# Scan of a Mamba-2 layer: the loads of the cumulated step sizes, one for each chunk, issued from ScalarE's queue rather than SyncE's

## The chip, the core and the metric

The kernel runs on one core of one Trainium2 chip. The metric is the device time of one execution in microseconds (us). The engines have these short names: PE is TensorE (matrix products), PEld its weight load, DVE is VectorE, ACT is ScalarE, POOL is GpSimd, SP is SyncE, which here does nothing but issue DMAs ("SPq" in the profile is its queue of issues).

## The reference

One inference step of a decoder trunk of two layers: a Mamba-2 SSD layer and a pooling layer, each with adaLN modulation, RMSNorm and a gate, on 1024 prompt tokens and 8 sequences of 8 sample tokens (1088 columns in all), model width 1024. The change lies in the scan of the SSD layer, which has 32 heads of 64 channels in 8 groups of 4 heads, a state of 128, and chunks of 128 tokens:

```python
def ssd_scan(x, dt, A, B, C, h0):
    ...
    acum = jnp.cumsum(dt * A.reshape(G, R), axis=2)          # per chunk: the cumulated step sizes
    seg = acum[:, :, :, None] - acum[:, :, None, :]
    decay = jnp.where(mask, jnp.exp(jnp.where(mask, seg, 0.0)), 0.0)
    CB = jnp.einsum('bctgn,bcsgn->bctsg', C, B)
    xdt = x * dt[..., None]
    y_intra = jnp.einsum('bctsgr,bcsgrp->bctgrp', CB[..., None] * decay, xdt)
    decay_end = jnp.exp(acum[:, :, -1:] - acum)
    chunk_states = jnp.einsum('bctgn,bctgr,bctgrp->bcgrpn', B, decay_end, xdt)
    chunk_decay = jnp.exp(acum[:, :, -1])
    # h <- chunk_decay * h + chunk_states, chunk by chunk, h_prev = the h ahead of each chunk
    y_inter = jnp.einsum('bctgn,bctgr,bcgrpn->bctgrp', C, jnp.exp(acum), h_prev)
    return y_intra + y_inter, h_final
```

All of it is float32. Products that must be exact to float32 are made as three products of high and low halves.

## The kernel before

**The scan.** Function `scan_group(g, T)` does one of the 8 head groups: 8 chunks of 128 prompt tokens, two at a time, and a ninth, shorter chunk with the 64 sample tokens. The cumulated step sizes of all heads lie in DRAM (`acd`, written once before the scan). For each chunk, `load_ac(c)` brings those of the group's 4 heads to the core, the same numbers to all 128 partitions, into a tile `acb` (128 x 4 x 128 float32, 256 KB; 128 KB for the ninth chunk). There are two buffers for `acb`. `front(c)` takes the tile of its chunk and first issues the load of the next chunk, which goes to the other buffer and so waits until the last reader of the chunk before is done. All readers of `acb` are on ACT: `ea` = exp(acb) (L543), four `M` = relu(tka - acb) (L556), and `cd` = exp of acb's last column (L574, only chunks 1 to 7). Beside them `front` transposes x and B on PE (L545, L549, tile `tr`), turns M into the decay matrix (ACT L557, DVE L559 and L560), makes `xd` (DVE L562), the copy `Bt` of the transposed B (ACT L566; L569 and L570 for the ninth chunk), and multiplies `ea` by C (DVE L575). `states` makes the chunk states `S` of two chunks on PE (L588, from `Bt` and `xd`) and carries the state on: `hd` = h x cd on POOL (L596), `h` = hd + S on DVE (L593, L597). `rows` makes the outputs on PE: L609 from `M`, L613 from `ea` and `h`; DVE adds them up (L580). The sample tokens follow (L617 to L667: `Z` L628, `st` L652 and L653, `xs` L660, S L663, store `hsT` L666), then the gate (`z` loads L512, L700, L701), the norm (L706 to L716, with a store `rsd` and a load `rs`) and the store of the result (`gyd`, L723).

**What runs beside it.** PE always has other products to make in between: the input projection of the next groups (`mm`, L182 to L184, a weight tile `wr` is loaded by SP at L117 to L123, split into `wh` by ACT at L139 and `wl` by DVE at L140; results are taken out by ACT at L419, the convolution is at L356 to L360), the adaLN vectors (`am` L253 and L262, with `mp` copied by ACT at L258), and, from the fifth group on, the output projection of the groups that are done (`gr` loaded at L737, split into `gh` by ACT L742 and `gl` by DVE L743; the running sum `x` is loaded at L1521, added to at L764, and stored as `x1d` at L1544). The table `FILL` says how many pieces of this other work are written between two steps of a scan.

**What sets the order.** The program is written once through this code, and a scheduler then gives each engine one fixed list of instructions. An engine works its list from the top: an instruction whose inputs or buffers aren't there holds up all that stands behind it on that engine. That holds for the DMAs too: a DMA stands in the list of the engine that issues it. The DMAs of SP and of ACT share eight completion semaphores, DMAHW0 to DMAHW7, which are given out in turn, and a DMA can be issued only when the DMA that had its semaphore before has landed. Before the change ACT issues no DMA; SP issues all of this stage.

Of the kernel before, what the change touches and what calls it, by code (L numbers as in the profile page):

```python
# [14 lines left out]
P = 128  # L15
# [82 lines left out]
class Build:  # L98
# [405 lines left out]
    def scan_group(self, g, T):  # L504
        nc, tk, gp, pp = self.nc, self.tk, self.gs, self.pp
# [18 lines left out]
        def load_ac(c):  # L524
            if c < 8:
                j, cc = c // 2, c % 2
                t = gp.tile([P, 4, 128], F32, tag="acb", bufs=2, name=self.name("acb"))
                nc.sync.dma_start(t, self.acd[32 * j + 4 * g:32 * j + 4 * g + 4, 128 * cc:128 * cc + 128].unsqueeze(0).to_broadcast([P, 4, 128]))
            else:
                t = gp.tile([P, 4, 128], F32, tag="acb", bufs=2, name=self.name("acb"))[:, :, :64]  # L530
                nc.sync.dma_start(t, self.acd[96 + 4 * g:100 + 4 * g, 256:320].unsqueeze(0).to_broadcast([P, 4, 64]))
            acbs[c] = t

        def front(c):
# [4 lines left out]
            tok = slice(t0, t0 + L)  # L539
            acb = acbs.pop(c)  # L540
            load_ac(c + 1) if c < 8 else None
            ea = gp.tile([P, 4, 128], F32, tag="ea", bufs=3, name=self.name("ea"))
            nc.scalar.activation(ea[:, :, :L], acb, AF.Exp)  # L543
# [112 lines left out]
        def state_sample(st, Bt, half):  # L656
# [10 lines left out]
            self.slots.free(hsl[half])  # L667

        load_ac(0)
        F = [front(0)]  # L670
        yield
# [1135 lines left out]
```

## Time and profile before

| | |
|---|---|
| median of 3 runs (lowest to highest) | 1624.79 us (1623.5 to 1626.45) |
| profiled execution, its own time | 1625.1 us |
| its span | 1623.2 us |
| granted TensorE clock, mean | 0.995 |
| PE busy / ACT busy, share of the span | 98% / 50% |
| the scan stage | about 355 to 930 us |
| loads of `acb` | 64 of 256 KB and 8 of 128 KB |

The span is the time from the first to the last instruction on the core; the execution's own time adds some 2 us around it. In the rows that follow, "busy" is the time in which an engine worked on an instruction, and a wait is the idle time of an engine ahead of an instruction, put down to the instruction or DMA that ended last of those it waited for. Waits of SPq are waits of the queue of issues.

### The profile page before, as it was taken

How to read it: one execution, taken by the hardware profiler on the slowest of the kernel's cores; microseconds unless marked ns; L12 is line 12 of the kernel's file. 1: busy time of each engine (PE TensorE's matmuls, PEld its weight loads, DVE VectorE, ACT ScalarE, POOL GpSimd, SP SyncE). 2: the span in 40 equal slices, each digit the busy share in tenths (PEclk: the TensorE clock that was granted, in tenths of full speed). 3: DMA queues.
4: the chain of work that ended last, by engine and by line, in shares of the span. 5: the costliest groups of instructions: out<-in, count | busy, mean ns of one | idle time of the engine just before them, and what ended most of it. 6: DMA issues, size and time to landing. Idle time of an engine off the chain costs nothing.

```text
span 1623.2 us, 30975 instructions
## 1 busy us (share of the span) xinstructions
PE 1594.8 (98%) x12061; PEld 1519.9 (94%) x12061; DVE 1290.4 (79%) x2140; ACT 815.2 (50%) x1565; POOL 497.8 (31%) x527
## 2 busy tenths in 40 slices
PE   8999999999999999999999999999999999999997
PEld 6899999998889898898899899999999999999997
DVE  6875779777787888889878867988899867577886
ACT  6653444357667667675555536632322233333364
POOL 0233556421221302120112222366667640000241
PEclk9999999999999999999999999999999999999999
DMA  9422232354554554678899633043333369665773
GB/s 348 163 99 82 94 110 71 107 198 128 194 161 159 166 190 134 215 226 295 272 333 313 216 130 112 29 143 111 103 108 100 134 206 362 181 159 182 160 175 121
DMA packets 122306, 275.60 MB, mean 170 GB/s; under 512 B 18192, under 2 KB 59312, under 8 KB 122160
## 3 DMA queue, kind: packets, MB, share of 16 engines
q1 hardware_dynamic: 118128, 260.91, 47.4%
q0 software_dynamic: 4032, 12.72, 4.5%
q8 instruction: 95, 1.56, 0.4%
q14 instruction: 51, 0.42, 0.1%
HBM read 201.12 MB, written 70.23 MB: 167 GB/s over the span
## 4 chain that ended last, share of the span: by engine, by line
PE 83%; DVE 6%; DMA 4%; issue 3%; ACT 3%; POOL 1%; SPq 0%; DVEq 0%; POOLq 0%; ACTq 0%
PE st L982 11%; PE st L980 11%; PE st L981 11%; PE mm L182 10%; PE mm L183 10%; PE mm L184 10%; PE op L1197 2%; PE op L1198 2%; PE op L1196 2%; PE y L609 2%; PE S L588 2%; PE y L613 1%; DMA acb<-acd 1%; PE am L253 1%; PE tr L549 1%
## 5 line engine op out<-in xcount | busy, mean ns | idle before, releaser
L982 PE MATMUL st<-hh,w 128*128 128x272 f32 x832 | 240.8, 289 | 2.3 <-DVE w L176 2.3
L980 PE MATMUL st<-hh,w 128*128 128x272 f32 x832 | 240.2, 289 | 0.0
L981 PE MATMUL st<-hl,w 128*128 128x272 f32 x832 | 239.8, 288 | 0.0
L982 PE MATMUL st<-t,w 128*128 128x272 f32 x624 | 179.5, 288 | 0.0
L980 PE MATMUL st<-t,w 128*128 128x272 f32 x624 | 179.5, 288 | 0.0
L981 PE MATMUL st<-t,w 128*128 128x272 f32 x624 | 179.2, 287 | 0.0
L182 PE MATMUL mm<-hh,wh 128*128 128x368 f32 (+1 forms) x528 | 178.2, 338 | 0.1
L183 PE MATMUL mm<-hl,wh 128*128 128x368 f32 (+1 forms) x528 | 173.4, 328 | 0.0
L184 PE MATMUL mm<-hh,wl 128*128 128x368 f32 (+1 forms) x528 | 173.4, 328 | 0.0
L174 ACT ACTIVATE w<-wr 128x512 fp32r<-128x512 f32 x104 | 65.7, 631 | 190.1 <-PE st L982 156.7
L982 PEld LDWEIGHTS st<-hh,w 128*128 128x128 f32 x832 | 156.4, 188 | 3.4 <-DVE w L176 3.4
L980 PEld LDWEIGHTS st<-hh,w 128*128 128x128 f32 x832 | 156.7, 188 | 0.3 <-issue 0.3
L981 PEld LDWEIGHTS st<-hl,w 128*128 128x128 f32 x832 | 156.8, 188 | 0.0
L596 POOL TENSOR_TENSOR hd<-h,cd 128x256 f32<-128x256 f32 x56 | 48.7, 870 | 347.8 <-DVE h L597 190.5
L182 PE MATMUL mm<-gh,wh 128*128 128x368 f32 (+1 forms) x384 | 129.1, 337 | 0.6 <-ACT raw L419 0.6
L1197 PE MATMUL op<-b,w 128*128 128x272 f32 x448 | 128.9, 288 | 0.7 <-DVE b L1126 0.7
L1196 PE MATMUL op<-b,w 128*128 128x272 f32 x448 | 129.4, 289 | 0.0
L1198 PE MATMUL op<-b,w 128*128 128x272 f32 x448 | 128.9, 288 | 0.0
L183 PE MATMUL mm<-gl,wh 128*128 128x368 f32 (+1 forms) x384 | 126.0, 328 | 1.1 <-DVE gl L743 1.0
L184 PE MATMUL mm<-gh,wl 128*128 128x368 f32 (+1 forms) x384 | 126.0, 328 | 0.0
L980 PEld LDWEIGHTS st<-t,w 128*128 128x128 f32 x624 | 117.7, 189 | 0.0
L982 PEld LDWEIGHTS st<-t,w 128*128 128x128 f32 x624 | 117.3, 188 | 0.0
(293 smaller groups left out, 4610.4 us busy)
## 6 DMA issues: line engine op xcount, KB each, us to landing
wr<-win SPq DMA_DIRECT2D x48, 512.0 KB, 3.9
acb<-acd SPq DMA_DIRECT2D x64, 256.0 KB, 4.0
wr<-pin SPq DMA_DIRECT2D x32, 512.0 KB, 3.8
wr<-pout SPq DMA_DIRECT2D x28, 512.0 KB, 3.9
x<-x1d SPq DMA_DIRECT2D x24, 544.0 KB, 6.6
x1d<-x SPq DMA_DIRECT2D x22, 544.0 KB, 5.5
wr<-pout POOLq DMA_DIRECT2D x20, 512.0 KB, 5.5
x<-xT SPq DMA_DIRECT2D x16, 544.0 KB, 6.1
```

The costliest lines, as they stand in the source:

```text
L174: self.nc.scalar.activation(hi, src, AF.Copy)
L182: nc.tensor.matmul(ps[:, :n], hi[:, k, :], ah[:, a:a + n], start=first, stop=False)
L183: nc.tensor.matmul(ps[:, :n], hi[:, k, :], al[:, a:a + n], start=False, stop=False)
L184: nc.tensor.matmul(ps[:, :n], lo[:, k, :], ah[:, a:a + n], start=False, stop=last)
L588: nc.tensor.matmul(S[:, 256 * i:256 * i + 256], Bt, xde.rearrange("p r q -> p (r q)"), start=True, stop=True)
L596: nc.gpsimd.tensor_tensor(out=hd, in0=h[-1], in1=cd.unsqueeze(2).to_broadcast([P, 4, 64]), op=ALU.mult)
L980: nc.tensor.matmul(ps[c][:, :QUART], hi[:, k], xh[:, t], start=(k == 0), stop=False)
L981: nc.tensor.matmul(ps[c][:, :QUART], hi[:, k], xl[:, t], start=False, stop=False)
L982: nc.tensor.matmul(ps[c][:, :QUART], lo[:, k], xh[:, t], start=False, stop=(k == 3))
L1196: nc.tensor.matmul(ps[:, :QUART], hi[:, k], xh, start=k == 0, stop=False)
L1197: nc.tensor.matmul(ps[:, :QUART], hi[:, k], xl, start=False, stop=False)
L1198: nc.tensor.matmul(ps[:, :QUART], lo[:, k], xh, start=False, stop=k == 7)
```

## The change

In `load_ac` the two DMAs are issued by ACT:

```diff
 def load_ac(c):
     if c < 8:
         j, cc = c // 2, c % 2
         t = gp.tile([P, 4, 128], F32, tag="acb", bufs=2, name=self.name("acb"))
-        nc.sync.dma_start(t, self.acd[32 * j + 4 * g:32 * j + 4 * g + 4, 128 * cc:128 * cc + 128].unsqueeze(0).to_broadcast([P, 4, 128]))
+        nc.scalar.dma_start(t, self.acd[32 * j + 4 * g:32 * j + 4 * g + 4, 128 * cc:128 * cc + 128].unsqueeze(0).to_broadcast([P, 4, 128]))
     else:
         t = gp.tile([P, 4, 128], F32, tag="acb", bufs=2, name=self.name("acb"))[:, :, :64]
-        nc.sync.dma_start(t, self.acd[96 + 4 * g:100 + 4 * g, 256:320].unsqueeze(0).to_broadcast([P, 4, 64]))
+        nc.scalar.dma_start(t, self.acd[96 + 4 * g:100 + 4 * g, 256:320].unsqueeze(0).to_broadcast([P, 4, 64]))
     acbs[c] = t
```

The 72 issues go from SP's list to ACT's (L528 and L531), and the scheduler arranges the lists of this stage anew; outside the stage the order stays. Of the three places shown here, each named by the time at which it lies in the profile before, the first is near the end of the last group (893 to 909 us). Numbers behind a name tell tiles of one kind apart; "waits" names the semaphores that the instruction waits for (DMAHW: a DMA's landing, PE, DVE, ACT as "Activation", POOL as "Pool": that engine's progress). ACT before, from the weight split `wh_10538` to the `Bt` of chunk 2 of the last group:

```order
L139 ACTIVATE wh_10538<-wr_10317 128x1024 [waits PE_49]
L556 ACTIVATE M_10621<-acb_10558,tka_1431 128x128 x4
L574 ACTIVATE cd_10634<-acb_10558 128x4 [waits Pool_49]
L574 ACTIVATE cd_10696<-acb_10612 128x4 [waits DMAHW2_49,Pool_49]
L557 ACTIVATE M_10621<-M_10621 128x512 [waits Activation_49]
L566 ACTIVATE Bt_10578<-tr_10562 128x128 [waits DVE_49,PE_49]
```

ACT now, at the same place:

```order
L528 DMA acb_10612<-acd 128x4x128 [waits DMAHW5_49]
L139 ACTIVATE wh_10538<-wr_10317 128x1024 [waits DMAHW4_49,PE_49]
L556 ACTIVATE M_10621<-acb_10558,tka_1431 128x128 x4
L574 ACTIVATE cd_10696<-acb_10612 128x4 [waits DMAHW5_49,Pool_49]
L557 ACTIVATE M_10621<-M_10621 128x512 [waits Activation_49]
L528 DMA acb_10674<-acd 128x4x128 [waits DMAHW0_49]
L566 ACTIVATE Bt_10578<-tr_10562 128x128 [waits DVE_49,PE_49]
```

Two loads now stand in ACT's list, one ahead of the weight split and one ahead of `Bt_10578`, and each waits for a semaphore that a DMA of SP had before it. These are SP's rows before, from the load of `x_10536` on (`x` is the running sum of the output projection, `rs` the norm's factors):

```order
L1521 DMA x_10536<-x1d_165 128x1088 [waits PE_49]
L666 DMA hsT<-h_189_10046 128x1024 [waits DVE_49,Pool_49]
L713 DMA rsd_127<-z_10092 4x272 [waits DMAHW4_49,Activation_49]
L1521 DMA x_10439<-x1d_164 128x1088 [waits DMAHW7_49,DMAHW5_49]
L117 DMA wr_10542<-wout 128x2x512 [waits DMAHW6_49]
L716 DMA rs_10395<-rsd_127 128x1088 [waits DMAHW4_49]
L528 DMA acb_10558<-acd 128x4x128 [waits DMAHW0_49,Activation_49]
L1521 DMA x_10699<-x1d_166 128x1088 [waits DMAHW1_49]
L528 DMA acb_10612<-acd 128x4x128 [waits DMAHW2_49,Activation_49]
L517 DMA h_208_10810<-h0T 128x1024 [waits DMAHW3_49,PE_49]
```

And SP now:

```order
L1521 DMA x_10536<-x1d_165 128x1088 [waits DMAHW3_49,PE_49]
L1544 DMA x1d_168<-x_9997 128x1088 [waits DMAHW4_49,DVE_49]
L1521 DMA x_10699<-x1d_166 128x1088 [waits DMAHW5_49]
L666 DMA hsT<-h_189_10046 128x1024 [waits DVE_49,Pool_49]
L713 DMA rsd_127<-z_10092 4x272 [waits DMAHW7_49,Activation_49]
L1521 DMA x_10439<-x1d_164 128x1088 [waits DMAHW4_49,DMAHW0_49]
L517 DMA h_208_10810<-h0T 128x1024 [waits DMAHW1_49,PE_49]
```

The `x_10699` of SP and the `acb_10612` of ACT have the same semaphore, DMAHW5, one after the other, and so have `x_10439` and `acb_10674` with DMAHW0. Some rows further down in ACT's list, before:

```order
L557 ACTIVATE M_10683<-M_10683 128x512 [waits Activation_49]
L556 ACTIVATE M_10735<-acb_10674,tka_1431 128x128 x4
L574 ACTIVATE cd_10748<-acb_10674 128x4 [waits Pool_49]
L557 ACTIVATE M_10735<-M_10735 128x512 [waits Activation_49]
L574 ACTIVATE cd_10807<-acb_10726 128x4 [waits DMAHW1_49,Pool_49]
L566 ACTIVATE Bt_10694<-tr_10678 128x128 [waits DVE_49,PE_49]
```

And now:

```order
L528 DMA acb_10726<-acd 128x4x128
L556 ACTIVATE M_10735<-acb_10674,tka_1431 128x128 x4
L574 ACTIVATE cd_10748<-acb_10674 128x4 [waits Pool_49]
L557 ACTIVATE M_10735<-M_10735 128x512 [waits Activation_49]
L531 DMA acb_10785<-acd 128x4x64 [waits Activation_49]
L566 ACTIVATE Bt_10694<-tr_10678 128x128 [waits DVE_49,PE_49]
L574 ACTIVATE cd_10807<-acb_10726 128x4 [waits DMAHW5_49,Pool_49]
```

Here `Bt_10694` and `cd_10807`, which reads the tile that has just been loaded, have changed places. The second place is ACT near 850 us, between the last group but one and the last; before:

```order
L556 ACTIVATE M_10104<-acb_10019,tka_1433 64x64 x4
L557 ACTIVATE M_10104<-M_10104 64x4x64 [waits Activation_49]
L566 ACTIVATE Bt_10039<-tr_10023 128x128 [waits DVE_49,PE_49]
L139 ACTIVATE wh_10153<-wr_9887 128x1024 [waits PE_49]
L742 ACTIVATE gh_10251<-gr_10173 128x1088 [waits DMAHW0_49,PE_49]
```

Now:

```order
L556 ACTIVATE M_10104<-acb_10019,tka_1433 64x64 x4
L528 DMA acb_10333<-acd 128x4x128 [waits DMAHW1_49]
L557 ACTIVATE M_10104<-M_10104 64x4x64 [waits Activation_49]
L528 DMA acb_10335<-acd 128x4x128 [waits DMAHW3_49]
L574 ACTIVATE cd_10436<-acb_10335 128x4 [waits DMAHW3_49,Pool_49]
L566 ACTIVATE Bt_10039<-tr_10023 128x128 [waits DVE_49,PE_49]
L139 ACTIVATE wh_10153<-wr_9887 128x1024 [waits PE_49]
```

The first two loads of the last group stand here now, and `cd_10436`, which needs the second of them, stands ahead of `Bt_10039`; before, it came 20 rows after it. The third place is DVE near 787 us, at the end of another group; before:

```order
L597 TENSOR_TENSOR h_9198<-hd_9199,S_9195 128x256 [waits PE_49,Pool_49]
L597 TENSOR_TENSOR h_9202<-hd_9203,S_9195 128x256 [waits Pool_49]
L559 TENSOR_TENSOR cb_9226<-tr_9212,kc 64x64 [waits PE_49]
...
L580 TENSOR_SCALAR xbc_8366<-xbc_8366,vec,y_9236 128x256 [waits PE_49]
L140 TENSOR_TENSOR wl_9276<-wr_9273,wh_9275 128x1024 [waits DMAHW2_49]
L631 TENSOR_TENSOR zsc_9266<-Z_9257,eap 128x256 [waits PE_49]
L653 TENSOR_TENSOR st_9339<-xd_9229,st_9339 64x256 [waits DVE_49,Activation_49]
```

Now:

```order
L597 TENSOR_TENSOR h_9198<-hd_9199,S_9195 128x256 [waits PE_49,Pool_49]
L140 TENSOR_TENSOR wl_9276<-wr_9273,wh_9275 128x1024 [waits DMAHW4_49,Activation_49]
L597 TENSOR_TENSOR h_9202<-hd_9203,S_9195 128x256 [waits Pool_49]
L559 TENSOR_TENSOR cb_9226<-tr_9212,kc 64x64 [waits PE_49]
...
L580 TENSOR_SCALAR xbc_8366<-xbc_8366,vec,y_9236 128x256 [waits PE_49]
L631 TENSOR_TENSOR zsc_9266<-Z_9257,eap 128x256 [waits PE_49]
L653 TENSOR_TENSOR st_9339<-xd_9229,st_9339 64x256 [waits DVE_49,Activation_49]
```

The weight split `wl_9276`, which waits for its weight tile and for ACT's half of the split, now stands ahead of the second state update and of the ninth chunk's `cb`, `xd` and `M`.

## The prediction

> **What bounds the kernel now.** I read the busy times of the page first, then busy times by stretches, then the waits of PE, ACT and SP inside the scan stage, then the loads themselves. The page's line of busy times:
>
> ```profile
> PE 1594.8 (98%) x12061; PEld 1519.9 (94%) x12061; DVE 1290.4 (79%) x2140; ACT 815.2 (50%) x1565; POOL 497.8 (31%) x527
> ```
>
> PE bounds the kernel as a whole. All 72 loads are issued between 356 and 905 us, and the lists of instructions differ only in that stage, so the busy times of it matter, and of two pieces in it. The columns are PE, PEld, DVE, ACT and POOL, then the granted PE clock, the DMA share and GB/s:
>
> ```profile
> 355.00:930.00 575.00, 568.51 (x4414) 515.10 (x4413) 475.57 (x786) 370.72 (x851) 109.64 (x164) 1.00 0.66 217
> 396.00:697.00 301.00, 300.96 (x2348) 270.38 (x2347) 248.28 (x379) 206.09 (x466) 62.70 (x109) 1.00 0.54 174
> 777.00:850.00 73.00, 71.31 (x548) 65.80 (x548) 61.01 (x117) 39.49 (x93) 11.12 (x11) 1.00 0.89 299
> ```
>
> In 575 us PE is idle for 575 − 568.51 = 6.5 us. That is the most that any change of waits in this stage can gain, at an unchanged PE work. ACT is idle for 575 − 370.7 = 204 us. Where those 6.5 us lie, by what PE waited for (total, times, longest):
>
> ```profile
> PE S L588 <- ACT Bt L566: 1.9, 1, 1.9
> PE y L613 <- DVE h L597: 1.0, 1, 1.0
> PE mm L183 <- DVE gl L743: 1.0, 1, 1.0
> PE y L613 <- DVE h L593: 0.8, 1, 0.8
> PE am L262 <- ACT mp L258: 0.6, 1, 0.6
> PE mm L182 <- ACT raw L419: 0.6, 1, 0.6
> PE tr L545 <- ACT Bt L566: 0.5, 1, 0.5
> ```
>
> Seven single waits, and no row names a load. The loads are late for ACT and in the way of SP, though:
>
> ```profile
> ACT cd L574 <- DMA acb<-acd: 13.1, 9, 3.9
> ACT ea L543 <- DMA acb<-acd: 5.8, 5, 2.4
> ```
>
> ```profile
> SPq L528 <- ACT M L556: 67.7, 28, 5.0
> SPq L528 <- ACT cd L574: 43.2, 15, 6.5
> SPq L528 <- ACT ea L543: 9.7, 5, 2.1
> SPq L528 <- DMA acb<-acd: 5.4, 3, 3.0
> ```
>
> SP stands for 126 us ahead of these loads, nearly always until ACT has read the old tile. The loads themselves (first and last issue, and how long one takes to land):
>
> ```profile
> L528 SPq DMA_DIRECT2D acb<-acd x64: 359/377/1062, 356.1 to 902.0; - x64
> L531 SPq DMA_DIRECT2D acb<-acd x8: 371/383/912, 386.4 to 904.3; - x8
> DMA to landing us min/median/max: 3.2/4.0/6.5
> ```
>
> **The change, part by part.** *Removed from SP:* 72 issues and the 126 us of waiting ahead of them. SP's other loads may go out earlier, but PE waits for a load of SP at one place only (the `gl` row), so little of it can be turned into time.
>
> *Added to ACT:* 72 issues of about 0.38 us, were they to cost what they cost SP (the trace shows no issue on ACT), 27 us of ACT's 204 idle. The wait for the buffer costs ACT nothing, since all readers of the old tile stand ahead on ACT itself. New is that ACT waits at an issue for the DMA that last had the same semaphore, and everything behind it in the list waits too.
>
> *Groups 1 to 4 of the scan* (396 to 697 us). PE is idle for 0.04 of 301 us, ACT for 301 − 206 = 95, or 24 a group. Nine issues add 9 × 0.38 = 3.4 us to a group. What hides them is ACT's idle time, since PE has other products queued. That is 24 / 9 = 2.7 us between two loads, seven times an issue. If at one place in each group ACT stood for a whole landing (4.0) at an issue, 4.0 − 2.7 = 1.3 us would be paid, 5 us over four groups. I take 0 (0 to +5).
>
> *The start.* The chain of waits there:
>
> ```profile
> 355.72 0.32 SPq L430
> 356.09 5.27 DMA acb<-acd
> ```
>
> The first load stood behind a store on SP that waited for ACT until 355.72; now ACT issues it by itself, 0.4 to 1.0 us earlier. The waits of 0.8 (`h` L593) and 0.5 (`Bt` L566, at 386 us, where `Bt` now stands ahead of the `ea` that waits for a load) both belong to this group: −0.9 (0 to −1.3).
>
> *Near 787 us,* the third place of the order, with what ACT, DVE and PE did there:
>
> ```profile
> 786.73 1.06 ACT L139 ACTIVATE wh<-wr 128x1024 fp32r<-128x1024 f32 x1 [3.51 <-DMA wr<-wout]
> 793.46 1.71 ACT L660 ACTIVATE xs<-st,kc 128x256 fp32r<-128x256 f32 x4 [4.20 <-DVE st L653]
> ```
>
> ```profile
> 785.85 0.42 DVE L597 TENSOR_TENSOR h<-hd,S 128x256 f32<-128x256 f32 x1 [0.79 <-POOL hd L596]
> 788.58 2.77 DVE L140 TENSOR_TENSOR wl<-wr,wh 128x1024 fp32r<-128x1024 f32 x1
> ```
>
> `wl` now stands ahead of the work from 785.85 to 788.58, 2.7 us, and can begin only when `wh` is done, at 787.8. So `wl` ends at 790.6, the 2.7 us come after it, and `st`, for which `xs` waits on ACT, is 0.8 + 2.7 − 0.8 = up to 2.7 us later; ahead of `mp`, for which PE already waits 0.6, more stands. I take +1.0 (0 to +2.7): the other products cover a part.
>
> *Near 841 us:*
>
> ```profile
> 833.16 7.92 DMA gr<-gyd
> ```
>
> This load ends the 1.0 of the `gl` row. A load of `acb` no longer stands ahead of it on SP: its issue is 0.38, its wait longer, so −0.7, between 0.38 and 1.0 (0 to −1.0).
>
> *Near 850 us,* the second place of the order, with ACT's rows and the step of the chain that needs `Bt`:
>
> ```profile
> 850.87 0.42 ACT L557 ACTIVATE M<-M 64x256 f32<-64x256 f32 x1
> 854.74 0.28 ACT L566 ACTIVATE Bt<-tr 128x128 f32<-128x128 f32 x1 [3.45 <-DVE xd L562]
> ```
>
> ```profile
> 856.48 0.86 PE S L588 x4
> ```
>
> Of the last group's two loads, the second stands behind the row at 850.87, so it is issued at 851.3 (850.87 + 0.42). It lands 4.0 to 6.5 later, 855.3 to 857.8; `cd` (0.2, by a row further on) and `Bt` (0.28) follow: 855.8 to 858.3, where PE took `Bt` at 856.48. So 0 to +1.8; I take +0.6, a landing of 5.25 halfway.
>
> *Near 893 us,* the first place. SP's issues there, the landing of the `x` loads (KB, us), what ACT did, and PE's need:
>
> ```profile
> 877.25 1.79 SPq L528 DMA_DIRECT2D acb<-acd  x2
> 886.40 0.38 SPq L528 DMA_DIRECT2D acb<-acd  x1
> 886.82 0.75 SPq L1521 DMA_DIRECT2D x<-x1d  x1
> 891.52 0.37 SPq L528 DMA_DIRECT2D acb<-acd  x1
> ```
>
> ```profile
> x<-x1d SPq DMA_DIRECT2D x16, 544.0 KB, 7.5
> ```
>
> ```profile
> 893.52 1.04 ACT L139 ACTIVATE wh<-wr 128x1024 fp32r<-128x1024 f32 x1
> 897.36 0.28 ACT L566 ACTIVATE Bt<-tr 128x128 f32<-128x128 f32 x1 [0.76 <-DVE xd L562]
> ```
>
> ```profile
> 897.72 0.86 PE S L588 x4
> ```
>
> `acb_10612`, now ahead of the `wh` of 893.52 on ACT, has the semaphore of the load of `x_10699` before it, which in turn has that of `acb_10478`, one of the two issues at 877.25. Landing after landing: 877.25 + 4.0 + 7.5 = 888.8, in time for 891.52; but with `x` issued at 886.82, as before, it lands at 894.3, ACT stands still until then, and `cd` waits for a load landing at 898.3 to 900.8, against a `Bt` that PE took at 897.72. The second pair: `acb_10558` at 886.40, + 4.0, `x_10439` + 7.5 = 897.9, and only then can ACT issue `acb_10674` and go on to this `Bt`, 898.6 instead of 897.64. Slack is 0.1 us here, so what comes late is paid. One pair costs 0 to 3.5, both 0 to 6; I take the middle, +3.0.
>
> *Near 908 us,* the last two changed rows of the first place:
>
> ```profile
> 907.78 0.21 ACT L574 ACTIVATE cd<-acb 128x4 f32<-128x4 f32 x1 [2.95 <-DMA acb<-acd]
> 907.89 0.26 ACT L566 ACTIVATE Bt<-tr 128x128 f32<-128x128 f32 x1
> ```
>
> `Bt`, for which PE waits 1.9, stood behind a `cd` that waited 2.95 for a load. Now it stands ahead: −1.9 (0 to −1.9). Next late is nothing that I can name.
>
> The remaining waits (`h` L597, `raw`) I leave at 0 (−1.5 to 0).
>
> The sum: −0.9 + 0 + 1.0 − 0.7 + 0.6 + 3.0 − 1.9 = +1.1. The profiled execution took 1625.1 us, 0.3 above the median of 1624.8, so 1626.2 there and 1625.9 as a median.
>
> A load takes 4.0 us to land in the median and 6.5 at most, and I kept both for ACT's queue, though the queue is another. The Trainium skill, page "DMA: Bandwidth & Descriptors", section "Issuing engines are not separate DMA queues", says that DMAs from any engine run on the same 16 DMA engines and that spreading them saves only the sequencer's time of initiating; by it the landings stay, as summed. The same page's section "Queues, rings and completion order" says that each DMA engine takes turns between the queue rows that have work for it, a packet at a time. No run shown here has two such queues of hardware DMAs; by this the small loads would pass SP's long ones.
>
> **The rivals.** *Faster: the gains come and the losses don't.* If a load on a queue of its own needn't stand in line behind SP's 544 KB transfers, it lands near 3.2, the shortest of before, rather than 4.0 to 6.5. Then the place at 850 us costs nothing (851.3 + 3.2 + 0.5 = 855.0), the pairs end earlier, and the start, `gr` and `Bt` give all they can: −1.3 − 1.0 − 1.9 = −4.2, or 1620.6. For it speaks that the DMA share is 0.89 from 777 to 850 us, so that standing in line is what makes landings long; against it that the same share is a limit of the DMA engines, whoever issues. This is what the taking of turns that the Trainium skill describes on the page "DMA: Bandwidth & Descriptors" would bring.
>
> *Slower: ACT and SP hand the semaphores to and fro.* Each ACT load waits for a load of SP that waited for an ACT load. It decides when SP's `x` loads go out less than 7.5 us ahead of the ACT issue that follows them, which holds for one of two pairs above. Then 6.0 near 893, 1.8 near 850 and 2.7 near 787 are paid, with half of the gains (−1.75): +8.75, or 1633.5. Against it: between 396 and 697 us the DMA share is lower (0.54), so standing in line is shorter.
>
> *Slower: an issue on ACT costs more.* At SP's longest, 1.06 rather than 0.38, nine issues take 6.1 us more in a group. If a quarter of it falls ahead of what PE waits for, 1.5 us in each of 8 groups, 12.2 in all: +13.3 or 1638.1. Against it: SP's 1.06 is the maximum of 64, the median 0.377.
>
> **How the numbers follow.** A measurement of this kernel can tell about 0.2% (3.25 us) from no change. The forecast, with its own range of −2 to +3, lies within that: 0.38. Faster: 0.20, since three gains must come whole. The semaphores: 0.27, as the price is paid at places with a slack of 0.1 us. The dear issue: 0.15. So faster 0.20, the same 0.38, slower 0.42. The range of 8 in 10 reaches from 1620.0, which leaves out the better third of the faster case, to 1637.0, which leaves out most of the dear issue's.
>
> **What would show it.** Right: PE's idle time in 355 to 930 us near 7.6 us; the wait of 1.9 at 908 us gone; ACT standing at L528 at 893 us, with its `wh` and `Bt` behind, and PE waiting for them; L528 rows on ACT's queue of about 0.38 us; no PE wait from 396 to 697 us. Wrong: rows of waits of PE between 396 and 697, which would say that ACT's float isn't what the busy times suggest; or landings near 3.2; or PE waits at places not listed here, since the lists were rearranged in many more.

## The result and the profile after

The changed kernel takes 1638.1 us in the median of 6 runs (1633.5 to 1645.2), the kernel before 1625.2 us in the runs beside it (1623.4 to 1626.5). The ratio is 1.0089, with a 95% interval of 1.0072 to 1.0106: slower by 0.9%, some 13 us. These six runs spread over 12 us and those of the kernel before beside them over 3; but later runs of the kernel before, taken beside the experiments, spread over 12 as well (1621.2 to 1633.1), so the spread isn't a mark of the change. The profiled execution, 1645.2 us, is the longest of the six; its span is 1643.0, 19.8 us over the 1623.2 of before.

The scan stage ends later now, so both kernels are read from 355 to 945 us here. The busy times of this stretch, before and then after (PE, PEld, DVE, ACT, POOL, granted clock, DMA share, GB/s):

```profile
355.00:945.00 590.00, 583.51 (x4505) 529.05 (x4504) 486.04 (x805) 376.81 (x860) 110.60 (x167) 1.00 0.65 215
```

```profile
355.00:945.00 590.00, 572.78 (x4387) 517.35 (x4385) 472.46 (x780) 369.13 (x849) 100.76 (x164) 0.98 0.63 212
```

PE is idle for 17.2 us instead of 6.5, which is 10.7 of the 19.8. The other part is in the clock: 0.98 over the stretch, where it was 1.00. Most of PE's waits after are for one thing (total, times, longest):

```profile
PE S L588 <- ACT Bt L566: 12.4, 6, 4.2
```

Of PE's timeline after, the five longest waits and a short one (in brackets, the idle time ahead):

```profile
369.08 1.22 PE L588 MATMUL S<-xd,Bt 128*128 128x256 f32 x2 [3.55 <-ACT Bt L566]
740.20 0.50 PE L182 MATMUL mm<-gh,wh 128*128 128x368 f32 x1 [2.25 <-ACT raw L419]
799.48 1.07 PE L628 MATMUL Z<-h,ctm 128*32 128x256 f32 x16 [1.64 <-issue]
843.49 0.70 PE L588 MATMUL S<-xd,Bt 128*128 128x256 f32 x2 [0.53 <-ACT Bt L566]
872.06 1.22 PE L588 MATMUL S<-xd,Bt 128*128 128x256 f32 x2 [4.21 <-ACT Bt L566]
918.00 1.22 PE L588 MATMUL S<-xd,Bt 128*128 128x256 f32 x2 [2.20 <-ACT Bt L566]
```

Two S products take 0.70 us behind the short wait and 1.22 behind three of the long ones. The busy times just behind the first show why (the columns as above):

```profile
370.00:375.00 5.00, 5.00 (x25) 3.73 (x25) 3.59 (x9) 3.50 (x11) 1.23 (x2) 0.50 0.31 90
```

The granted clock is 0.50 there, half of full speed. Read in short pieces, half of the time in which PE works at that clock comes to 3.06, 1.71, 2.45 and 1.67 us behind the four waits of 2.2 us and more, 8.9 in all; behind the 1.64 at 799 us the clock stays at 1.00. So 10.7 of idle time and 8.9 of clock make 19.6 of the 19.8.

The loads after, with the landings, and what ACT waits for from them:

```profile
L528 ACTq DMA_DIRECT2D acb<-acd x64: 366/366/530, 355.4 to 923.7; - x64
DMA to landing us min/median/max: 3.1/4.6/11.2
```

```profile
ACT cd L574 <- DMA acb<-acd: 36.7, 12, 9.6
ACT ea L543 <- DMA acb<-acd: 5.5, 2, 3.0
ACT M L556 <- DMA acb<-acd: 3.8, 2, 2.3
```

An issue costs ACT 0.37 us, no more than it cost SP. But a load lands after up to 11.2 us, where it was 6.5, and ACT waits 46 us for loads instead of 19. How that reaches PE, in ACT's timeline ahead of the longest wait:

```profile
859.80 0.37 ACTq L528 DMA_DIRECT2D acb<-acd  x1
861.59 0.37 ACTq L528 DMA_DIRECT2D acb<-acd  x1
...
871.63 0.21 ACT L574 ACTIVATE cd<-acb 128x4 f32<-128x4 f32 x1 [9.63 <-DMA acb<-acd]
871.75 0.26 ACT L566 ACTIVATE Bt<-tr 128x128 f32<-128x128 f32 x1
```

The `cd` of the load issued last stands next in ACT's list; it waits 9.63 us, `Bt` behind it is done at 872.0, and PE goes on at 872.06.

### The profile page after: what moved, and what is told of

It is laid out like the page before. It is cut to its first block, busy times and chain, and to the rows that moved or that the text cites. A ratio compares the mean times of both kernels' runs of the same rounds, so it can differ in the third digit from the quotient of the medians.

```text
span 1643.0 us, 30930 instructions
## 1 busy us (share of the span) xinstructions
PE 1603.6 (98%) x12061; PEld 1525.2 (93%) x12061; DVE 1292.0 (79%) x2140; ACT 816.0 (50%) x1565; POOL 490.1 (30%) x527
## 3 DMA queue, kind: packets, MB, share of 16 engines
q8 instruction: 95, 1.56, 0.4%
## 4 chain that ended last, share of the span: by engine, by line
PE 80%; DVE 7%; DMA 6%; issue 3%; ACT 2%; POOL 1%; SPq 0%; ACTq 0%; DVEq 0%; POOLq 0%
PE st L982 11%; PE st L980 11%; PE st L981 10%; PE mm L182 10%; PE mm L183 9%; PE mm L184 9%; DMA acb<-acd 3%; PE op L1197 2%; PE op L1198 2%; PE op L1196 2%; PE y L609 2%; PE S L588 2%; PE y L613 1%; PE am L253 1%; PE tr L549 1%
```

## The experiments

Two theories stand against each other at first. *Order:* ACT's list now has a reader of a load that has only just been issued ahead of work that PE needs. *Transfer:* the landings themselves are later, since a load on ACT's queue shares the DMA engines with what SP issues after it.

**`cd` pinned behind `Bt`.**

```diff
-                nc.scalar.activation(Bt, pt[:, 256:384], AF.Copy)
+                bt = nc.scalar.activation(Bt, pt[:, 256:384], AF.Copy)
...
-                nc.scalar.activation(cd, acb[:, :, 127], AF.Exp)
+                with self.tc.issue_after(bt.ins): nc.scalar.activation(cd, acb[:, :, 127], AF.Exp)
```

> The changed kernel, with each cd (L574) queued on ScalarE behind the Bt copy of its own chunk; nothing else is pinned. Order theory: ScalarE stands at a cd whose load has only just been issued and the Bt that PE needs stands behind it; then the PE waits for Bt, 12.4 us in the profile of the changed kernel, fall under 4 us, the halved clock at 872 and 918 us goes, and the time is 1624 to 1629 us. Transfer theory: it is the late landing itself (up to 11.2 us instead of 6.5) that costs; whatever reads acb first then stands instead, PE still waits for 8 us or more, and the time stays at 1634 or above. Rest-of-the-order theory (other moved instructions on DVE and SP): 1634 or above with PE's waits at other lines than Bt.

Measured: 1674.8 us, ratio 1.0300 (1.0285 to 1.0315), far worse than either theory had. Waits of PE and of ACT in the stage:

```profile
PE S L588 <- ACT Bt L566: 30.6, 10, 5.2
```

```profile
ACT ea L543 <- DMA acb<-acd: 94.7, 32, 12.2
```

The pin did more than it was meant to. `cd` is also the last reader of the old `acb`; behind `Bt` it holds back the next load, so `ea` waits for that one. ACT's list was arranged anew elsewhere too, so the whole of the 3.0% can't be put down to this. It tells nothing of the order theory as put. It does show that on ACT a load stands in the list behind the last reader of the old tile: it goes out as soon as `cd` is done (920.55 us in the longest case), and `ea`, next in the list, waits up to 12.2 us for it.

**The same order, other rows.** The step sizes are stored so that the four heads of a chunk lie side by side; a load is then 128 rows of 2 KB rather than 512 of 512 B. The lists of all engines keep their order, but for two more stores of the step sizes, made before the scan.

```diff
-        nc.sync.dma_start(self.acd, ac)
+        [nc.sync.dma_start(self.acd[c], ac[:, 128 * c:128 * c + n]) for c, n in enumerate((128, 128, 64))]
...
-                nc.scalar.dma_start(t, self.acd[32 * j + 4 * g:32 * j + 4 * g + 4, 128 * cc:128 * cc + 128].unsqueeze(0).to_broadcast([P, 4, 128]))
+                nc.scalar.dma_start(t.rearrange("p r n -> p (r n)"), self.acd[cc][32 * j + 4 * g:32 * j + 4 * g + 4].rearrange("r n -> (r n)").unsqueeze(0).to_broadcast([P, 512]))
```

> The changed kernel, with the cumulated step sizes stored so that the 4 heads of a chunk lie in one piece of DRAM: a load is 128 rows of 2 KB rather than 512 rows of 512 B; the order of every engine is as in the changed kernel. Transfer theory (a queue of its own shares the DMA engines row by row, and small rows lose against SP's rows of 4 KB): the median landing falls from 4.6 to under 3.8 us and the longest from 11.2 to under 7.5, ScalarE's waits for acb from 45.9 to under 25 us, the time to 1626 to 1631. Order theory: a landing cannot fall under some 3 us, so ScalarE still stands at cd with Bt behind; half or more of the loss stays: 1632 to 1638.

Measured: 1627.9 us, ratio 1.0016 (1.0006 to 1.0026). PE's waits for `Bt`, ACT's for `cd`, and the landings:

```profile
PE S L588 <- ACT Bt L566: 3.1, 5, 1.2
```

```profile
ACT cd L574 <- DMA acb<-acd: 28.2, 11, 5.9
...
DMA to landing us min/median/max: 3.0/4.6/7.3
```

With the order of the changed kernel, four fifths of the loss are gone. The transfer theory had the time and the longest landing right, but not the median, which stays at 4.6, nor ACT's waits (39.5 us in all, where under 25 was expected). What went is the tail, the landings over 7.3 us: PE waits for `Bt` at most 1.2 at a time here, where behind the one of 11.2 it waited 3.55 and lost the clock. No piece from 355 to 985 us shows a clock under 1.00 in this profile. It is of the fastest of these twelve runs (1624.9 us), though, as that of the changed kernel is of its slowest, so the two profiles set side by side make the difference larger than the medians do. The control, the same storage with the loads on SP:

> The kernel before, with the step sizes stored as in the run with rows of 2 KB; the loads stay on SyncE and the order of every engine is that of before. Transfer theory: on one queue the small rows cost little, so the time stays within 1623 to 1626, and what moving the loads costs with wide rows is the 1627.9 of the moved ones less this, 2 to 4 us. Rival (wide rows make the whole stage faster, and hid a loss of the move that is still there): 1616 to 1621.

1627.3 us, ratio 1.0009 (0.9995 to 1.0023): the storage by itself changes nothing that can be told. So the change costs 0.9% with rows of 512 B, and with rows of 2 KB nothing that these two runs tell apart (1.0016 against 1.0009). No version here beats the kernel before.

**The queue by itself.** A program that only loads: the 256 KB of step sizes once or twice, and four loads of 544 KB on SP.

```diff
+        cases = {"spalone": ("s", 0), "actalone": ("a", 0), "spahead": ("s", 4), "actbeside": ("a", 4), "spbehind": ("b", 4), "sptwo": ("ss", 4),
+                 "acttwo": ("aa", 4), "actwide": ("A", 4), "spwide": ("S", 4)}
...
-        Build(tc, io).run()
+        bench(tc, nc, io)
```

> Not the trunk: it leaves the whole computation out and only loads. In each of nine cases, three times over, the 256 KB load of the step sizes goes out alone or together with four loads of 544 KB on SyncE's queue. Transfer theory: on ScalarE's queue beside the four it lands 3 us or more later than on SyncE's queue ahead of the four (some 7 to 9 us against 4), two at once later still (10 or more), with rows of 2 KB beside the four at most 6; alone, both queues take the same. Rival (the queue makes no difference, as all run on the same DMA engines): beside and ahead agree within 1 us. Rival (a queue of its own passes the long loads): beside lands no later than alone plus 0.5 us.

Measured, median landings of a load (KB, us):

```profile
bspalone<-acd SPq DMA_DIRECT2D x3, 256.0 KB, 3.1
bactalone<-acd ACTq DMA_DIRECT2D x3, 256.0 KB, 3.1
bspahead<-acd SPq DMA_DIRECT2D x3, 256.0 KB, 4.9
bspbehind<-acd SPq DMA_DIRECT2D x3, 256.0 KB, 7.4
bactbeside<-acd ACTq DMA_DIRECT2D x3, 256.0 KB, 5.9
bactwide<-acc ACTq DMA_DIRECT2D x3, 256.0 KB, 5.6
```

Two loads at once, first on SP ahead of the four, then on ACT beside them; a copy by DVE marks the landing of each:

```profile
204.28 0.93 SPq L1802 DMA_DIRECT2D bsptwo<-acd  x2
...
209.54 0.17 DVE L1817 COPY tok<-bsptwo 128x4 f32<-128x4 f32 x1 [1.34 <-DMA bsptwo<-acd]
...
220.89 0.99 ACTq L1802 DMA_DIRECT2D bacttwo<-acd  x2
...
231.63 0.17 DVE L1817 COPY tok<-bacttwo 128x4 f32<-128x4 f32 x1 [4.90 <-DMA bacttwo<-acd]
```

Alone, the queues are alike. One load beside the four (`actbeside`) lands 1.0 us later than ahead of them on SP (`spahead`), not 3, and 1.5 earlier than behind them (`spbehind`): a queue of its own is worth something to a load that would else stand behind the long ones, and costs something where it would have stood ahead. Two land after 10.7 us instead of 5.3. Of the same size is the 11.2 of the changed kernel at its start, where ACT issues two loads at 355.4 and SP four long ones within the next 4 us. In these runs the loads that were issued first on SP's queue landed first; beside SP's queue, loads that SP issued later held up those of ACT. Rows of 2 KB against 512 B, in a second program of the kind:

> Not the trunk: it leaves the whole computation out and only loads, as in the run with nine cases. Two loads at once, or one beside eight long ones, with rows of 512 B or of 2 KB. Transfer theory (a queue of its own gets a turn for each row, so its time goes by the number of rows while SyncE has rows to send): two loads on ScalarE's queue land the second after about 10 us with 512 B and 6 to 7 us with 2 KB; on SyncE ahead of the four, 5 us with either. One load beside eight long ones: 6 us, as beside four. Rival (the bytes decide, not the rows): no difference between 512 B and 2 KB.

```profile
32.65 0.80 SPq L1800 DMA_DIRECT2D bsptwowide<-acc  x2
...
38.96 0.17 DVE L1817 COPY tok<-bsptwowide 128x4 f32<-128x4 f32 x1 [1.74 <-DMA bsptwowide<-acc]
...
54.85 0.98 ACTq L1802 DMA_DIRECT2D bacttwo<-acd  x2
...
65.63 0.17 DVE L1817 COPY tok<-bacttwo 128x4 f32<-128x4 f32 x1 [4.79 <-DMA bacttwo<-acd]
...
76.34 0.85 ACTq L1800 DMA_DIRECT2D bacttwowide<-acc  x2
...
85.02 0.17 DVE L1817 COPY tok<-bacttwowide 128x4 f32<-128x4 f32 x1 [3.73 <-DMA bacttwowide<-acc]
```

From the issue of two loads to the landing of the second, in the median of the repeats of both programs: on ACT's queue 10.7 us with narrow rows (10.6 to 10.8) and 7.8 with wide ones (8.7, 7.7, 7.8); on SP's, ahead of the four, 5.3 with narrow rows (4.7 to 5.7) and 6.2 with wide ones (6.2 to 6.3). So on ACT's queue the rows matter, by 2.9 us where 3 to 4 were expected; on SP's the wide ones were slower, where 5 was expected for both. What the move to ACT's queue costs hangs on the rows: 5.4 us with narrow ones, 1.6 with wide ones. One load beside eight long ones took 5.9 with narrow and 5.7 with wide rows, as beside four.

**Which loads.** First the first load of each group put back on SP, so that ACT issues no two close together at a group's start:

```diff
-                nc.scalar.dma_start(t, self.acd[32 * j + 4 * g:32 * j + 4 * g + 4, 128 * cc:128 * cc + 128].unsqueeze(0).to_broadcast([P, 4, 128]))
+                (nc.scalar if c else nc.sync).dma_start(t, self.acd[32 * j + 4 * g:32 * j + 4 * g + 4, 128 * cc:128 * cc + 128].unsqueeze(0).to_broadcast([P, 4, 128]))
```

> The changed kernel, with the first load of each of the 8 groups back on SyncE, so that ScalarE no longer issues two loads close together at the start of a group; 64 of 72 loads stay on ScalarE. Transfer theory (two loads close together on a queue of their own, beside SyncE's long ones, are what takes 10 us): the waits of 3.55 us at 369 and 4.21 us at 872 go, no landing takes more than 8 us, the time is 1627 to 1631. Order theory (ScalarE's list as rearranged, whichever load it is): 1634 to 1638.

1636.8 us, ratio 1.0065 (1.0042 to 1.0089): by the medians the pairs hold a quarter of the loss, but the intervals overlap, and the order theory's range of 1634 to 1638 held. The wait at 872 us went and that at 369 fell to 2.2, but a single load landed after 10.6 us, against the transfer theory, and PE waited 3.5 at 839 and 4.2 at 911. The pair is one way to a late landing, not the only one. The scheduler arranged the lists anew in this version and the next two, so they place the loss only roughly. Then the loads of groups 0 to 4 alone, and of groups 5 to 7 alone, on ACT (`nc.scalar if g < 5 else nc.sync`, and the reverse):

> Loads of groups 0 to 4 on ScalarE, of groups 5 to 7 on SyncE. By the profile of the changed kernel, groups 0 to 4 hold 7 us at the start (3.55 idle and 3.4 by the halved clock) and 2.8 in four short waits, less 1.3 that went: the time is 1630 to 1634, some 60% of the loss. Rival (the loss comes where the DMA engines are full, from 705 us on, with the output projection's loads): 1625 to 1628.

> The counterpart of the run with groups 0 to 4: loads of groups 5 to 7 on ScalarE, of groups 0 to 4 on SyncE. Transfer theory: most of what the change costs lies where SyncE's queue has most to send, from 705 us on; with 0.31% for groups 0 to 4 of 0.89% in all, 0.4 to 0.7% here, 1630 to 1636, with landings of 6 to 10 us from 700 us on and at most 6.5 before. If the loss were an interplay of both parts of the scan, under 0.3%.

1.0031 (1.0013 to 1.0049) and 1.0040 (1.0025 to 1.0056): together 0.71%, against 0.89% (0.72 to 1.06) for all; groups 0 to 4 hold about a third rather than the 60% that were expected. Landings in the stretch that each moves, 355 to 396 us of the first and 700 to 945 us of the second:

```profile
DMA to landing us min/median/max: 3.4/5.3/11.2
```

```profile
DMA to landing us min/median/max: 3.3/7.3/9.1
```

Before, the second stretch had a median of 5.4 and 6.5 at most. The loss is in both parts of the scan; that of the first includes a wait of 2.13 at 738 us, where no load moves (see `raw` below).

**`Bt` taken off ACT.** VectorE copies it, behind its own `xd`:

```diff
-                nc.scalar.activation(Bt, pt[:, 256:384], AF.Copy)
+                nc.vector.tensor_copy(Bt, pt[:, 256:384])
```

> The changed kernel, with the Bt copies of the prompt chunks made by VectorE right behind the work that they wait for, not by ScalarE; so a ScalarE that stands at a load holds up no Bt. Order theory (a landing that is late costs time only because Bt stands behind the waiting cd on ScalarE): PE waits little for Bt, no halved clock from it, 1624 to 1630 us, with the landings still at 4.6 in the median and over 9 at the longest. Transfer theory alone (the landings themselves decide, whatever stands behind): PE waits for M or ea instead of Bt, 10 us or more in all, 1633 to 1640.

> The kernel before (loads on SyncE), with the Bt copies made by VectorE. Control for the run with the changed kernel: 56 copies of some 0.28 us are 16 us more on VectorE, which is busy for 476 of 575 us. If that is hidden, 1622 to 1626, the waits of 1.9 at 908 and 0.5 at 386 us gone; if VectorE is late for xd, 1628 or more, and the run beside it must be read against this one.

1.0113 (1.0092 to 1.0134) with the loads on ACT, 1641.4 us, and 1.0053 (1.0036 to 1.0070) with them on SP, 1632.3. VectorE's copies cost 0.5% by themselves, so the first must be read against the second: the move still costs 9.1 us. PE's waits with the loads on ACT:

```profile
PE S L588 <- DVE Bt L566: 5.4, 5, 2.9
PE mm L183 <- DVE gl L743: 2.3, 1, 2.3
PE y L613 <- DVE h L597: 1.5, 1, 1.5
PE y L609 <- DVE M L560: 1.3, 1, 1.3
```

The longest wait for `Bt`, in ACT's, DVE's and PE's timelines:

```profile
919.46 0.63 ACT L543 ACTIVATE ea<-acb 128x512 f32<-128x512 f32 x1 [6.02 <-DMA acb<-acd]
...
920.64 0.69 DVE L560 TENSOR_TENSOR M<-M,cb 128x512 f32<-128x512 f32 x1 [4.11 <-ACT M L557]
...
922.18 0.70 PE L588 MATMUL S<-xd,Bt 128*128 128x256 f32 x2 [2.92 <-DVE Bt L566]
```

The narrow order theory falls: `Bt` stands behind no waiting `cd` here, and the late load still reaches PE. ACT waits 6.02 for it at `ea`, DVE waits 4.11 for the `M` that ACT makes next, and `Bt`, which DVE copies behind that, is late; `h` and `M` themselves are waited for elsewhere. So all that ACT does stands behind the load, and so does what others make of it. Of the 0.5% of the copies little shows as PE's idle time (5.0 us in the stage with the loads on SP, 6.7 before); where it goes stays open.

**The clock by itself.** PE works in blocks, and waits for VectorE in between for a time that is set:

> Not the trunk: it leaves the whole computation out. PE works in blocks of some 12 us, and between two blocks it waits for VectorE for a time that is set, 11 lengths from about 0.7 to 6 us, three times over. Clock theory: up to about 1.9 us the granted clock stays 1.00; from about 2.2 us on it goes to 0.50, for 3 us or more after PE starts again. If the halved clock in the changed kernel has another cause (the load on the chip, the transfers), it stays 1.00 here at every length.

```profile
112.71 15.78 PE L1792 MATMUL ps<-r,k 128*128 128x256 f32 x72 [1.85 <-DVE r L1795]
130.55 17.47 PE L1792 MATMUL ps<-r,k 128*128 128x256 f32 x72 [2.06 <-DVE r L1795]
...
188.94 17.45 PE L1792 MATMUL ps<-r,k 128*128 128x256 f32 x72 [2.89 <-DVE r L1795]
...
332.48 15.78 PE L1792 MATMUL ps<-r,k 128*128 128x256 f32 x72 [2.06 <-DVE r L1795]
```

None of 18 waits up to 1.85 us was followed by a longer block; of 9 between 2.06 and 2.53 us 5 were, by 1.7 us, and all waits of 2.9 and 3.4 were. The same 2.06 us did it once and not the next time. No transfer runs here, so it is PE's idle time. Which of two equal waits does it is in the trace too. The stretches at half clock begin a whole number of steps of 3.41 us apart (130.88, 151.36 and 188.91 us: 6 and 11 steps). Here is the step ahead of each of the two waits of 2.06 us, up to where the next one begins, and what follows the first (PE, PEld, DVE, POOL, clock, DMA share, GB/s):

```profile
127.47:130.88 3.41, 1.35 (x7) 0.90 (x6) 1.81 (x3) 0.00 (x0) 1.00 0.00 0
130.88:134.29 3.41, 3.41 (x10) 2.70 (x9) 0.00 (x0) 0.00 (x0) 0.50 0.00 0
...
328.86:332.27 3.41, 1.56 (x8) 1.03 (x6) 1.74 (x3) 0.00 (x0) 1.00 0.00 0
```

The first wait lies in one step, in which PE is busy for 1.35 us, and the next step runs at half clock. The second runs on into the next step; PE is busy for 1.56 us, and the clock stays. Behind the first block, each of the 10 steps of this program in which PE was busy for under 40% was followed by one at 0.50, and none of the others (43% and more) was. Last, the changed kernel once more:

> The changed kernel once more, to see how far its time goes with the clock of PE. If PE's clock halves after an idle stretch and only some executions reach that length, this one's time above 1625 equals PE's added idle time plus half of the time at half clock, to 1 us; if the clock plays no part, the time follows the idle time alone.

1640.4 us, span 1638.3, 15.1 over before. From 355 to 985 us PE is idle for 14.1 us in it (before 6.7) and loses 5.0 by the clock: 12.4. Another 2.5 lies ahead of the scan (0.4 idle, 2.0 by the clock), where the kernels are alike. So the sum, 14.9, holds to 0.2 us over both stretches, and the clock is one part of the spread from run to run. The longest landing was 11.3 this time.

## Why the prediction was wrong, step by step

The forecast was 1625.9 us with a range to 1637.0; 1638.1 lies above it.

*The landing.* The step that failed is the one that kept 4.0 to 6.5 us for a load "though the queue is another". Landings reached 11.2. The rival of a queue of its own that lands loads at 3.2 had the sign wrong. The text had allowed for a gain, that a small load would pass SP's long ones, and for no loss; but a load that stood ahead of long ones in the one queue has nothing to pass. At the start it stood so, issued at 356.1 by SP with the long ones from 357.6 on. The rule that the Trainium skill gives on the page "DMA: Bandwidth & Descriptors", section "Queues, rings and completion order", that a DMA engine takes turns between queue rows, agrees with the programs that only load, in which two loads beside four long ones took 10.7 us on ACT's queue and 5.3 ahead of them on SP's.

*The clock.* Every term was priced as idle time. The four waits over 2 us cost nearly twice their idle time at most: 8.9 us of the 19.8 in the profile. The trace of before had nothing to show it in this stage, but it had behind the stage:

```profile
1018.88 0.43 PE L182 MATMUL pl<-hh,wh 128*128 128x352 f32 x1 [1.92 <-ACT hh L319]
```

The clock is 0.50 for 3.4 us behind that wait, so the price could have been read there.

*The signs that it named.* PE's idle time from 355 to 930 us is 17.2 us, not near 7.6. L528's issues cost 0.37, as said, and the wait at 908 us is gone. ACT's stand at L528 at 893 us didn't come. Of the signs of being wrong two came: waits of PE between 396 and 697 us, and waits at places that aren't listed.

*The start,* −0.9 forecast: the load went out 0.7 us earlier (355.4 against 356.1), but the second one landed after 11.2 us; 3.55 idle and 3.1 by the clock came in place of 1.3.

*Groups 1 to 4,* 0 (0 to +5): five waits of 0.2 to 1.3 us, 2.8 in all, all for `Bt`. In the bounds, but the prediction had called any such row a sign against its view of ACT's idle time.

*Near 787,* +1.0: the number was right, the first steps too, the end in part by luck. DVE stood for `wl` until `wh` was there, `h` came after it, and PE waited 1.64 at 799, for `h` ahead of `Z`; forecast was a longer wait for `mp`, for which it had waited 0.6:

```profile
797.82 1.23 DVE L140 TENSOR_TENSOR wl<-wr,wh 128x1024 fp32r<-128x1024 f32 x1 [2.11 <-ACT wh L139]
798.96 0.41 DVE L597 TENSOR_TENSOR h<-hd,S 128x256 f32<-128x256 f32 x1
```

`wh`, and so `wl`, was late because ACT had stood 3.95 us at a `cd` for a load, which the sum didn't have.

*Near 908,* −1.9: the wait is gone from PE's list, as said. *Near 841,* −0.7: the row was misread. The wait for `gl` stood at 734 us, not behind the `gr` load of 833:

```profile
734.01 0.44 PE L183 MATMUL mm<-gl,wh 128*128 128x368 f32 x1 [0.95 <-DVE gl L743]
```

It is gone as well, but the wait for `raw` (below) came 6 us later. What stood near 841 was the 1.0 for `h` at 847, left at 0; that is gone too. *Near 850,* +0.6 (0 to +1.8): the place was right, `cd` ahead of `Bt`; with a landing of 10.0 instead of 5.25 it cost 4.21, and 2.5 by the clock. *Near 893,* +3.0: PE waited 2.20 at 918 and lost 1.7 by the clock, which is near the number, but by luck. ACT never stood at an issue for a semaphore: each of the 72 issues in its timeline begins while the instruction ahead of it on ACT is still at work. `acb_10612` went out at 909.6, during such an `ea`, and landed 7.4 us later, beside loads of SP. The rival of the semaphores falls with it.

*The dear issue* came out nearest by its time (1638.1) and is refuted by its row: 0.366 us in the median, 0.530 at most. *`raw`,* left at 0, cost 2.25 at 740 us and 1.7 by the clock; in that trace ACT stands there at `gh` for loads of `gr`. The move isn't needed for it: with all loads on SP and wide rows PE waited 2.46 at 734, with only groups 0 to 4 moved 2.13 at 738, and the same changed kernel waited 1.20 in its second profile. So this part of the loss in the profile may be no more than the spread from run to run.

*What stays open.* With wide rows the loads still land at 6.3 us in the median from 700 us on (before 5.4) and cost next to nothing. That only the tail counts is read from the waits, was not tested by itself, and isn't the whole: the 7.4 us of `acb_10612` cost 2.20 and 1.7, and the 7.3 of the wide rows at most 1.2. Where in ACT's list the reader stands when a load is late counts too.

## What to carry to other kernels

A DMA moved to another engine's queue leaves its place in line: ahead of long loads on one queue it landed first here, and beside them it was held up by what was issued later, more so in rows of 512 B than of 2 KB. Look at which transfers follow it within a landing's time, not only at what an issue costs and who waits for the queue. On an engine that works its list in order, a load and its first reader want other work between them. And where PE is the bound, price a wait of some 2 us and more with the clock that it can cost.

## What the runs showed of the hardware that was not expected

The granted clock halved after idle stretches of PE far shorter than the 3.4 us that a step of it lasts. In the clock program, behind the first block, it did so never up to 1.85 us (18 waits), in 5 of 9 cases between 2.06 and 2.53 us and always from 2.9 us on. The length of the wait alone doesn't decide, and these bounds don't hold for the trunk: there it halved after 1.92 us (before, at 1018.9) and not after 2.39 (the changed kernel's second profile, at 913.7). What fits both is PE's busy share within a step. In the changed kernel's profile, too, the stretches at half clock begin whole steps of 3.41 us apart (368.38, 740.43, 870.14 and 917.92 us: 109, 38 and 14 steps), and PE had been busy for 0.56 to 1.29 us of the step ahead of each. Behind the 1.64 us at 799, where the clock stayed, the wait fell across two steps with 2.80 and 2.39 us of work. It then stays at 0.50 for one step, a price of 1.7 us if PE works all through it, or for two where PE isn't kept busy in the first (at 368 and 870 us). The Trainium skill, page "TensorE: Matmul & The Clock Gate", Part 1, gives half rate after an idle window of about 3.4 us, in a window that runs free of the kernel. The steps of 3.41 us and the free running agree with that; a window that is idle throughout wasn't needed here, one with PE busy for under 40% was enough.
